# Late modulation vectors as row products, decay columns in the value block, token norms without VectorE

## The chip, the cores and the metric

The kernel runs on one core of a Trainium2 chip. Its time is device microseconds of one launch. Five engines work side by side, each through its own queue in order: TensorE (matmuls, transposes), VectorE, ScalarE, GpSimd, and SyncE (SP), which here only issues transfers. Data lie in HBM, in SBUF (128 partitions) and in PSUM, where matmuls accumulate.

## What is computed

One layer of a hybrid diffusion backbone on 512 latent tokens with 256 context tokens, D_MODEL 1024, float32 in and out:

```python
mod_lat = silu(c) @ w_mod + b_mod            # 6 vectors of 1024
sh1, sc1, g1, sh2, sc2, g2 = split(mod_lat, 6)
hx = rms_norm(x) * (1 + sc1) + sh1           # hc: the same of ctx, by mod_ctx
ak, av, qkv, db, da, aq, z, gate = split_cols(hx @ w_in)   # hc: the first five
attn = latent_attention(rope(rms(aq)), [k_ctx; k_lat], [v_ctx; v_lat])
q, k, v = silu(conv3(qkv)); q = l2(q) * 128**-0.5; k = l2(k)   # per head of 128
beta = sigmoid(db); log_a = -exp(a_log) * softplus(da + dt_bias)
gdn = rms(gated_delta_rule(q, k, v, log_a, beta), both directions) * silu(z)
y = sigmoid(g_a) * (attn @ w_pa) + sigmoid(g_d) * (gdn @ w_pd)
x = x + g1 * (y @ w_out)
h2 = rms_norm(x) * (1 + sc2) + sh2
u = conv3(h2 @ w_up); x = x + g2 * ((silu(u_g) * u_v) @ w_down)
out = rms_norm(x, final_norm_w)
```

The early vectors sh1 and sc1 are needed at once; g1, sh2, sc2 and g2 (4096 columns of w_mod, 16 MB) only from the output projection on: the late modulation vectors.

## The kernel before

Every large product is made of three fp32r matmuls (`mm3`): each operand is split into a high part (a copy on ScalarE, `whi`) and a low part (a subtraction on VectorE, `wlo`), and high x high, high x low and low x high are summed in PSUM. `load_w` loads a 128x1024 block of weights (512 KB, SP's queue) and splits it; it has three slots for split blocks.

The work runs in this order. (1) Up to 70 us: early modulation, norms and transposes of x and ctx, `hx` and `hc` (channels on partitions). (2) The key/value/query stage, `for blk in range(6)`: a 256-column block of keys (blk 0, six token tiles), of values (blk 1, six tiles), four of queries (four tiles each). A tile is 24 matmuls into `pq` with tokens on partitions; keys and queries then get their rope on VectorE and are transposed back (`columns`). Two side jobs are stepped in between: `next(mods)`, 2.6 steps per tile, and `next(dec)` at the tiles named in `DAT`. (3) Attention, with delta-rule projections between its steps. (4) The delta rule by four pairs of heads (`gdn_solve`, `gdn_inv`, `gdn_scan`), with projections, and from about 732 us the output projections `w_pa` and `w_pd`, woven in by rates (`weave`, `filler`). In a scan step the products `r` on VectorE stand between two groups of matmuls, and projection matmuls are put there as cover. (5) `w_out`, the MLP (`w_up`, `w_down`), the last norm.

TensorE's order is kept as written (`pinned`); that of other engines is set by a scheduler with priorities (`first`, `sooner`), except where `keep_in_program_order` is called.

`late_mods` (lines 367 to 399) takes the 4096 late columns in eight groups of 512 and each group in eight slices of 128 rows of w_mod: 64 loads of 256 KB. Odd slices are multiplied by silu(c) and summed on VectorE (`macc`, line 377), even ones scaled on ScalarE (line 379) and summed on GpSimd (line 381); `total` sums over the partitions with a matmul by ones, `columns` turns the 512 sums into four columns by one-row transposes, and VectorE adds the bias.

`decays` (line 596) projects `hc` and `hx` to the 32 columns db, da by 48 matmuls with the 32 weight columns as the stationary side, copies the result out (`grow`), transposes it by six tiles, and computes beta, the decays and their sums.

`tokens(h, part, src)` transposes a head's q, k or v to tokens on partitions; ScalarE squares and sums (`kss`). For q the factor `rkq` and for k the factors `rkk` and `hks` come from it: VectorE adds and scales, GpSimd raises to -1/2 (`rsqrt`), VectorE scales again. `hks` scales the v of the same head.

`finish_pa` and `finish_pd` apply the sigmoid gates to a chunk of 128 channels; `tdr` in HBM holds the gates and the first branch's result in between (store `tdr<-ga`).

Of the kernel before, what the change touches and what calls it, by code (L numbers as in the profile page):

```python
# [48 lines left out]
MV, MT, CT = 0, 6, 9  # L49
MACT, MK, MU = 1, 2.6, 0  # L50
MPIN, MB = 1, 5
DA = '11142332'
DAT = [(int(DA[i]), int(DA[i + 1])) for i in range(0, 8, 2)]
# [22 lines left out]
R_QW, R_QS, R_KW, R_KS, R_A, R_DT, R_END = 0, 128, 256, 384, 512, 528, 544  # L76


def hybrid_layer_body(tc, x, ctxt, xT, consts, cols, rows, w_mod1, w_mod2, w_db, w_aq, w_cm, w_pa, w_pd, w_out,
# [54 lines left out]
    with es:  # L134
# [27 lines left out]
        col = cp.tile([P, S_END + 120], F32, name="col")[:, 0:S_END]  # L162
# [5 lines left out]
        V.memset(mhalf, -0.5)  # L168
        mod = cr.tile([P, 48], F32, name="mod")
        modc = cp.tile([P, 16], F32, name="modc")  # L170
        csl = cp.tile([P, KT], F32, name="csl")
# [24 lines left out]
        def load_w(src, nk=KT, pool=None, bufs=OH):  # L196
# [3 lines left out]
            n = nk * P  # L200
# [85 lines left out]
        def tokens(h, part, src):  # L286
# [77 lines left out]
        def held(i):  # L364
            return tc.keep_in_program_order(i) if MPIN else i

        def late_mods():
            accs = {}

            def part(q, k):  # L370
                if k == 0:
                    accs[q] = [mdp.tile([P, 512], F32, name="macc", tag="macc", bufs=4) for _ in range(2)]
                av, ap = accs[q]
                wk = mdp.tile([P, 512], F32, name="wmd", tag="wmd", bufs=MB)
                SP.dma_start(wk, w_mod2[q, k // 2][:, (k % 2) * 512:(k % 2) * 512 + 512])
                if k % 2:
                    held(V.scalar_tensor_tensor(out=av, in0=wk, scalar=csl[:, k:k + 1], in1=av, op0=ALU.mult, op1=ALU.add))  # L377
                else:
                    held(A.activation((av, ap, wk)[min(k // 2, 2)], wk, AF.Copy, scale=csl[:, k:k + 1]))
                    if k > 2:  # L380
                        held(G.tensor_tensor(out=ap, in0=ap, in1=wk, op=ALU.add))
                if k == KT - 1:
                    held((V if MV else G).tensor_tensor(out=ap, in0=ap, in1=av, op=ALU.add))

            def total(q):
                ps = xbank()[0:1, :, :].rearrange("p a b -> p (a b)")
                mm(ps, ones[:, 0:1], accs[q][1])
                act(accs[q][0][0:1, :], ps)

            def columns(q):  # L390
                pst = xbank()[:, 0, 0:4]
                for i in range(4):
                    T.transpose(pst[:, i:i + 1], accs[q][0][0:1, i * P:(i + 1) * P], ident[0:1, 0:1])
                tt(mod[:, 16 + 4 * q:20 + 4 * q], pst, col[:, S_BMOD + 16 + 4 * q:S_BMOD + 20 + 4 * q], ALU.add)

            for i in range(9 * KT + CT - 7):
                for at, fn in ((MT, total), (CT, columns)):
                    q = (i - KT - at) // KT
                    if (i - at) % KT == 0 and 0 <= q < 8:
                        fn(q)  # L400
                if i < 8 * KT:
                    part(i // KT, i % KT)
                yield

        modact, mods = [MACT], late_mods()
# [14 lines left out]
        with m1_es:  # L420
# [38 lines left out]
            V.tensor_copy(csl, cs.rearrange("p (k two) -> p k two", two=2)[:, :, 0])  # L459
# [136 lines left out]
        def decays(g1):  # L596
            rowt = g1.tile([P, 32], F32, name="rowt")
            SP.dma_start(rowt, rows[R_A:R_END].partition_broadcast(P))
# [3 lines left out]
            raw = g1.tile([P, 256], F32, name="dbraw")  # L602
            SP.dma_start(raw, w_db)
            dbh = g1.tile([P, 256], F32R, name="dbh")
            dbl = g1.tile([P, 256], F32R, name="dbl")
            split(dbh, dbl, raw)
            grow = g1.tile([32, NA], F32, name="grow")
            for (xh, xl, n, off) in ((hcH, hcL, NCX, 0), (hxH, hxL, NL, NCX)):
                ps = mbank()[0:32]
                for k in range(KT):  # L610
                    mm3(ps[:, 0:n], dbh[:, k * 32:(k + 1) * 32], dbl[:, k * 32:(k + 1) * 32], xh[:, k, :], xl[:, k, :], k, KT)
# [990 lines left out]
```

## Time and profile before

| what | value |
|---|---|
| median of three runs | 1276.62 us (1276.61 to 1277.89) |
| profiled execution | 1276.79 us, its span 1275.0 us |
| TensorE matmul busy | 1217.5 us |
| VectorE busy | 849.0 us |
| ScalarE busy | 624.2 us |
| GpSimd busy | 308.5 us |

The times of the profile run from the span's start. PE is TensorE, PEld its loading of weights, DVE VectorE, ACT ScalarE, POOL GpSimd, SPq the queue of SyncE. A line number is that of kernel.py; most are those of small helpers, so groups go by the names of tiles.

### The profile page before, as it was taken

The page shows a single profiled execution, that of the slowest core. Times are in us where ns is not written, and L with a number is a line of the kernel's source. Part 1 is how long each engine was busy: PE and PEld are TensorE (multiplying, and loading weights), DVE is VectorE, ACT ScalarE, POOL GpSimd, SP SyncE. Part 2 cuts the span into 40 slices and gives each one's busy share as a digit, 9 for nine tenths or more (in the row PEclk, how much of TensorE's full clock was granted, in tenths as well). Part 3 has the DMA queues.
Part 4 walks back from the last instruction along what each step waited for, and adds up shares of the span by engine and source line. Part 5 has one row for each costly group of instructions (what it writes and reads, how often), then busy time and mean ns, then how long its engine had stood idle before and what let it go on. Part 6 is the DMA issues. An engine that isn't in the chain of part 4 may idle for free.

```text
span 1275.0 us, 20851 instructions
## 1 busy us (share of the span) xinstructions
PE 1217.5 (95%) x7835; PEld 1027.1 (81%) x7835; DVE 849.0 (67%) x1625; ACT 624.2 (49%) x1403; POOL 308.5 (24%) x364
## 2 busy tenths in 40 slices
PE   8899999999988899999999999999999999999996
PEld 4487878898877778778888888788988888888886
DVE  5886987777769985876665756565766666653333
ACT  5453657666666665474453543333444444442231
POOL 1753430000024348758547400000000000000000
PEclk8999999999999999999999999999999999999998
DMA  8656641111254643533543663464133222333321
GB/s 320 225 170 215 224 130 63 67 71 54 88 187 136 186 129 121 194 115 126 183 127 129 193 197 118 147 232 133 33 116 99 93 92 98 99 95 91 104 91 66
DMA packets 70788, 170.79 MB, mean 134 GB/s; under 512 B 7872, under 2 KB 18720, under 8 KB 69280
## 3 DMA queue, kind: packets, MB, share of 16 engines
q1 hardware_dynamic: 70688, 169.47, 40.3%
q8 instruction: 61, 1.00, 0.3%
q14 instruction: 39, 0.32, 0.1%
HBM read 144.23 MB, written 25.21 MB: 133 GB/s over the span
## 4 chain that ended last, share of the span: by engine, by line
PE 70%; DVE 12%; DMA 5%; ACT 3%; POOL 3%; issue 2%; SPq 0%; POOLq 0%; DVEq 0%; ACTq 0%
PE mc L87 32%; PE mb L87 20%; PE pb L87 5%; PE pq L87 3%; PE pS L87 3%; PE ab L87 3%; DVE wlo L108 2%; DMA Gb<-gamdr 2%; PE ab L91 1%; DMA M<-gamdr 1%; DVE macc L377 1%; PE pk L87 1%; PE xb L91 1%; DVE qt L108 1%; POOL prod L108 1%
## 5 line engine op out<-in xcount | busy, mean ns | idle before, releaser
L108 DVE TENSOR_TENSOR wlo<-wraw,whi 128x1024 fp32r<-128x1024 f32 x152 | 188.3, 1240 | 162.9 <-ACT whi L120 159.9
L120 ACT ACTIVATE whi<-wraw 128x1024 fp32r<-128x1024 f32 x152 | 158.8, 1047 | 208.4 <-PE mc L87 103.4
L87 PE MATMUL mc<-h,whi 128*128 128x512 f32 (+1 forms) x752 | 219.5, 376 | 0.3 <-ACT whi L120 0.3
L87 PE MATMUL mb<-hxH,whi 128*128 128x512 f32 x384 | 163.7, 426 | 2.6 <-DVE R L108 2.1
L87 PEld LDWEIGHTS mc<-h,whi 128*128 128x128 f32 x752 | 138.0, 188 | 26.0 <-ACT whi L120 0.5
L87 PE MATMUL mb<-hxH,wlo 128*128 128x512 f32 x384 | 153.7, 400 | 0.0
L87 PE MATMUL mb<-hxL,whi 128*128 128x512 f32 x384 | 153.0, 398 | 0.0
L87 PE MATMUL mc<-h,wlo 128*128 128x512 f32 (+1 forms) x376 | 141.3, 376 | 0.5 <-DVE wlo L108 0.5
L108 POOL TENSOR_TENSOR rc<-rc,mhalf 128x2 f32<-128x2 f32 x4 | 3.2, 811 | 452.3 <-DVE rc L114 452.3
L87 PE MATMUL mc<-a,whi 128*128 128x512 f32 (+1 forms) x396 | 111.1, 366 | 0.6 <-DVE x L117 0.6
L87 PEld LDWEIGHTS mb<-hxH,wlo 128*128 128x128 f32 x384 | 73.7, 192 | 17.0
L87 PEld LDWEIGHTS mb<-hxH,whi 128*128 128x128 f32 x384 | 74.0, 193 | 13.9 <-ACT t L120 2.3
L87 PEld LDWEIGHTS mb<-hxL,whi 128*128 128x128 f32 x384 | 74.3, 194 | 10.0
L87 PEld LDWEIGHTS mc<-a,whi 128*128 128x128 f32 x396 | 71.6, 189 | 12.9 <-DVE x L117 0.8
L87 PEld LDWEIGHTS mc<-h,wlo 128*128 128x128 f32 x376 | 70.8, 188 | 13.7 <-DVE wlo L108 1.0
L87 PE MATMUL mc<-a,wlo 128*128 128x512 f32 (+1 forms) x198 | 72.3, 365 | 0.0
L117 DVE SCALAR_TENSOR_TENSOR u<-mc,col,u 128x511 f32<-128x511 f32 x88 | 65.3, 746 | 1.4
L108 POOL TENSOR_TENSOR prod<-X,R 128x31 f32<-128x31 f32 (+15 forms) x93 | 55.4, 596 | 21.1 <-DVE X L108 14.3
L108 POOL TENSOR_TENSOR R<-R,prod 128x31 f32<-128x31 f32 (+15 forms) x93 | 54.9, 590 | 6.9
L87 PE MATMUL pq<-whi,hxH 128*128 128x256 f32 x192 | 55.3, 288 | 0.0
L87 PE MATMUL pq<-wlo,hxH 128*128 128x256 f32 x192 | 53.5, 279 | 0.2 <-DVE wlo L108 0.2
L87 PE MATMUL pq<-whi,hxL 128*128 128x256 f32 x192 | 53.4, 278 | 0.0
(346 smaller groups left out, 2859.4 us busy)
## 6 DMA issues: line engine op xcount, KB each, us to landing
wraw<-in_w_cm_dram SPq DMA_DIRECT2D x48, 512.0 KB, 4.1
wraw<-in_w_up_dram SPq DMA_DIRECT2D x44, 512.0 KB, 3.7
wmd<-in_w_mod_dram SPq DMA_DIRECT2D x64, 256.0 KB, 3.7
wm<-in_w_mod_dram SPq DMA_DIRECT2D x8, 1024.0 KB, 8.7
wraw<-in_w_down_dram SPq DMA_DIRECT2D x16, 512.0 KB, 3.6
wraw<-in_w_aq_dram SPq DMA_DIRECT2D x12, 512.0 KB, 4.7
M<-gamdr SPq DMA_DIRECT2D x64, 64.0 KB, 4.4
wraw<-in_w_pa_dram SPq DMA_DIRECT2D x8, 512.0 KB, 4.1
```

What stands on the lines that cost most here:

```text
L87: i = nc.tensor.matmul(*a, **k)
L91: i = nc.tensor.transpose(*a, **k)
L108: (eng or V).tensor_tensor(out=out, in0=a, in1=b, op=op)
L117: V.scalar_tensor_tensor(out=out, in0=a, scalar=s, in1=b, op0=op0, op1=op1)
L120: A.activation(out, a, f, **kw)
L377: held(V.scalar_tensor_tensor(out=av, in0=wk, scalar=csl[:, k:k + 1], in1=av, op0=ALU.mult, op1=ALU.add))
```

## The change

Three parts. `late_mods` is new: the weights are laid out transposed (`w_mod2[j]`: 128 output columns on partitions, 1024 inputs along the row), silu(c) is broadcast to all partitions (`cw`), and one VectorE instruction per 128 columns multiplies the two and gives the row's sum as a column of `ms`: 32 loads of 512 KB and 32 products. They are stepped from the output projections by `more_mods`, with rates .25 per head step in `w_pa`, .14 in `w_pd` and .25 per step in `w_out`, into a pool of its own (`lm`, two row buffers) that opens after `hx` closes.

The 32 columns db, da are put behind the 256 value columns: the value block is 288 wide, its weights come in three pieces (864, 864 and 576 columns), and columns 256 to 288 of each tile are copied to `psc`. The separate projection and its transposes are gone, and the steps of `decays` stand at other tiles.

In `tokens`, the additions and scalings are ScalarE's (Identity with scale and bias), `hks` is a power 1/2 on GpSimd, and the factor 128**-0.5 of q is put into the power. Besides, `finish_pd` has one addition on GpSimd instead of VectorE, and the tiles of `two` have another alignment.

```diff
-MV, MT, CT = 0, 6, 9
-MACT, MK, MU = 1, 2.6, 0
-MPIN, MB = 1, 5
-DA = '11142332'
+MPA, MPD, MPO = .25, .14, .25
+DA = '203242'
...
+        half6 = cpad[:, S_END:S_END + 6]
+        G.memset(half6, 0.5)
+        epss = {v: cpad[:, S_END + 6 + i:S_END + 7 + i] for i, v in enumerate((1.0, 4.0, 512.0))}
...
         def two(pool, k, by, name):
-            t = pool.tile([P, 2 * k * NL + 128], F32R, align_bytes=2048, name=name)
+            t = pool.tile([P, 2 * k * NL + 64], F32R, align_bytes=512, name=name)
...
                     if part != 2:
-                        rr = (rkq, rkk)[part][h]
-                        rsqrt(rr, kss[:, 0:n], 1.0, 4 * EPS)
+                        rr, q = (rkq, rkk)[part][h], (128.0, 1.0)[part]
+                        act(rr, kss[:, 0:n], AF.Identity, scale=q, bias=epss[4 * q])
+                        tt(rr, rr, mhalf[:, 0:n], ALU.pow, G)
                     if part == 1:
-                        stt(hks[h], kss[:, 0:n], 4 * EPS, rr, ALU.add, ALU.mult)
-                        ts(hks[h], hks[h], 0.5, ALU.mult)
-                    if part == 0:
-                        ts(rr, rr, 128.0 ** -0.5, ALU.mult)
+                        act(hks[h], kss[:, 0:n], AF.Identity, scale=0.25, bias=epss[1.0])
+                        tt(hks[h], hks[h], half6, ALU.pow, G)
...
+            SP.dma_start(cw, rows[R_C:R_END].partition_broadcast(P))
+            th = row()
+            act(th, cw, AF.Tanh, scale=0.5)
+            stt(cw, th, 1.0, cw, ALU.add, ALU.mult)
+            yield
+            for j in range(32):
+                wl = row()
+                SP.dma_start(wl, w_mod2[j])
+                tc.keep_in_program_order(V.scalar_tensor_tensor(out=wl, in0=wl, scalar=0.5, in1=cw, op0=ALU.mult, op1=ALU.mult,
+                                                                accum_out=ms[:, j:j + 1]))
+                if j % 8 == 7:
+                    tt(mod[:, 9 + j:17 + j], ms[:, j - 7:j + 1], col[:, S_BMOD + 9 + j:S_BMOD + 17 + j], ALU.add)
                 yield
...
+        def more_mods(rate):
+            mcount[0] += rate
+            while mcount[0] >= 1:
+                mcount[0] -= 1
+                next(mods, None)
...
-            raw = g1.tile([P, 256], F32, name="dbraw")
-            SP.dma_start(raw, w_db)
...
-                for k in range(KT):
-                    mm3(ps[:, 0:n], dbh[:, k * 32:(k + 1) * 32], dbl[:, k * 32:(k + 1) * 32], xh[:, k, :], xl[:, k, :], k, KT)
-                V.tensor_copy(grow[:, off:off + n], ps[:, 0:n])
-            yield
-            psc = flat(xbank())[:, 0:192].rearrange("p (a b) -> p a b", b=32)
-            for t in range(6):
-                T.transpose(psc[:, t, :], grow[:, t * P:(t + 1) * P], ident[0:32, 0:32])
+            psc = g1.tile([P, 6, 32], F32, name="psc")
+            yield psc
...
             for blk in range(6):
-                w2 = [load_w(w_aq[blk, i]) for i in range(2)]
+                if blk == 1:
+                    w2 = [load_w(w_av[:, 864 * i:864 * i + 288 * n], n=288 * n) for i, n in ((0, 3), (1, 3), (2, 2))]
+                else:
+                    w2 = [load_w(w_aq[max(blk - 1, 0), i]) for i in range(2)]
...
                     if blk == 1:
-                        split(VH[:, t, :], VL[:, t, :], pq)
+                        split(VH[:, t, :], VL[:, t, :], pq[:, 0:256])
+                        V.tensor_copy(psc[:, t, :], pq[:, 256:288])
                         continue
...
-            for _ in mods:
-                pass
...
             hx_es.close()
+            lmp.append(lm_es.enter_context(tc.tile_pool(name="lm", bufs=1, side="right", reuse_waits="tile")))
+            next(mods)
...
-                tt(gd, gd, ga, ALU.add)
+                tt(gd, gd, ga, ALU.add, G)
...
-        def head_gemm(ps, w, xs):
+        def head_gemm(ps, w, xs, rate):
             for h in range(NH):
                 while xs[h] is None:
                     yield
                 head_steps(ps, w, xs, h)
+                more_mods(rate)
                 yield
```

`paired` calls `more_mods(rate)` in the same way behind each `head_steps`, and `out_proj` calls `more_mods(MPO)` behind each of its eight steps.

## Rows read from the trace of the kernel before

**Rows 1.** The page: busy time, share of the span, instructions.

```profile
PE 1217.5 (95%) x7835; PEld 1027.1 (81%) x7835; DVE 849.0 (67%) x1625; ACT 624.2 (49%) x1403; POOL 308.5 (24%) x364
```

**Rows 2.** Windows by stage: length; PE, PEld, DVE, ACT, POOL busy; clock, DMA.

```profile
70.00:184.00 114.00, 107.40 (x829) 93.54 (x828) 99.45 (x260) 62.39 (x182) 45.93 (x34) 1.00 0.61 197
...
732.00:805.00 73.00, 71.99 (x498) 62.27 (x493) 43.22 (x94) 25.21 (x53) 0.00 (x0) 1.00 0.46 149
805.00:852.00 47.00, 46.24 (x203) 36.77 (x202) 28.95 (x47) 16.29 (x33) 1.64 (x1) 1.00 0.57 183
852.00:877.00 25.00, 25.00 (x111) 20.65 (x110) 13.80 (x19) 8.74 (x13) 0.00 (x0) 1.00 0.62 212
```

**Rows 3.** Chain of waits, 58 to 190 us: start, length, what (pieces of a kind).

```profile
70.48 5.77 PE pq L87 x48
...
97.82 8.29 PE mb L87 x48
...
108.83 0.95 PE xb L87 x2
109.77 2.94 PE pq L87 x24
112.71 0.33 PE xb L91 x4
...
115.98 0.48 PE xb L91 x6
...
172.75 0.22 PE pt L91 x2
...
183.50 0.44 PE pt L91 x2
```

**Rows 4.** Groups on VectorE, 70 to 184 us: busy us, mean ns, idle before.

```profile
L377 DVE SCALAR_TENSOR_TENSOR macc<-wmd,csl,macc 128x512 f32<-128x512 f32 x32 | 28.9, 908 | 1.1 <-DMA wmd<-in_w_mod_dram 1.1
```

**Rows 5.** Chain of waits, 758 to 770 us.

```profile
764.05 2.06 PE mb L87 x9
```

**Rows 6.** Waits of PE, 70 to 190 us: total us, times, longest.

```profile
PE pq L87 <- DVE wlo L108: 1.6, 2, 1.4
```

**Rows 7.** Groups on VectorE, 184 to 620 us: the forms behind the sums of q.

```profile
L112 DVE TENSOR_SCALAR rkq<-rkq 128x4 f32<-128x4 f32 x8 | 4.3, 543 | 6.6 <-POOL rkq L108 6.6
...
L114 DVE TENSOR_SCALAR rkq<-gkss 128x4 f32<-128x4 f32 x8 | 3.6, 455 | 12.7 <-ACT xb L120 12.7
```

**Rows 8.** Chain of waits, 345 to 700 us.

```profile
366.23 1.67 DVE hk L112
...
470.75 1.84 DVE rkq L114
```

**Rows 9.** Groups on ScalarE, 70 to 184 us.

```profile
L120 ACT ACTIVATION_READ_ACCUMULATOR qtmp<-pq 128x1 f32 x44 | 8.7, 197 | 0.0
```

**Rows 10.** Tile rkk: durations in ns, least/median/most, first and last start.

```profile
L108 POOL TENSOR_TENSOR rkk<-rkk,mhalf x8: 1321/1330/1971, 199.8 to 417.5; 128x6 f32<-128x6 f32 x8
```

**Rows 11.** Tile qt.

```profile
L108 DVE TENSOR_TENSOR qt<-qt,qtmp x20: 406/411/1506, 83.3 to 182.7; 128x256 f32<-128x256 f32 x20
```

**Rows 12.** Groups on VectorE, 805 to 852 us.

```profile
L108 DVE TENSOR_TENSOR wlo<-wraw,whi 128x1024 fp32r<-128x1024 f32 x8 | 9.8, 1220 | 2.9 <-ACT whi L120 2.9
L108 DVE TENSOR_TENSOR gd<-gd,ga 128x512 f32<-128x512 f32 x7 | 4.8, 689 | 0.2
```

**Rows 13.** Tile macc.

```profile
L377 DVE SCALAR_TENSOR_TENSOR macc<-wmd,csl,macc x32: 731/741/1705, 74.5 to 173.3; 128x512 f32<-128x512 f32 x32
```

**Rows 14.** Timeline of VectorE, 763 to 768 us: start, length, instructions.

```profile
763.87 1.11 DVE L117 SCALAR_TENSOR_TENSOR r<-pb,eg,vtok 128x128 f32<-128x128 f32 x4
```

**Rows 15.** The page's DMA issues: KB each, us to landing.

```profile
wraw<-in_w_pa_dram SPq DMA_DIRECT2D x8, 512.0 KB, 4.1
```

**Rows 16.** Waits of SP's queue, 690 to 880 us: total us, times, longest.

```profile
SPq L1246 <- DVE ga L117: 30.9, 7, 8.9
```

**Rows 17.** Groups on GpSimd, 70 to 184 us.

```profile
L383 POOL TENSOR_TENSOR macc<-macc 128x512 f32<-128x512 f32 x8 | 11.3, 1410 | 13.1 <-DVE macc L377 8.0 <-DVE qsc L114 5.0
```

More of the change, by code (lines that the diff above doesn't have):

```diff
@@ L48 @@
 NS = 2
-MV, MT, CT = 0, 6, 9
-MACT, MK, MU = 1, 2.6, 0
-MPIN, MB = 1, 5
-DA = '11142332'
-DAT = [(int(DA[i]), int(DA[i + 1])) for i in range(0, 8, 2)]
+MPA, MPD, MPO = .25, .14, .25
+DA = '203242'
+DAT = [(int(DA[i]), int(DA[i + 1])) for i in range(0, len(DA), 2)]
 KPIN, LAG, FQ = 1, 3, 0
@@ L75, with hybrid_layer_body @@
 S_BMOD, S_CW, S_FW, S_FB, S_GNW, S_FNW, S_C, S_END = 0, 48, 120, 252, 296, 297, 305, 321
-R_QW, R_QS, R_KW, R_KS, R_A, R_DT, R_END = 0, 128, 256, 384, 512, 528, 544
-def hybrid_layer_body(tc, x, ctxt, xT, consts, cols, rows, w_mod1, w_mod2, w_db, w_aq, w_cm, w_pa, w_pd, w_out,
+R_QW, R_QS, R_KW, R_KS, R_A, R_DT, R_C, R_END = 0, 128, 256, 384, 512, 528, 544, 1568
+def hybrid_layer_body(tc, x, ctxt, xT, consts, cols, rows, w_mod1, w_mod2, w_av, w_aq, w_cm, w_pa, w_pd, w_out,
                       w_up, w_down, outT, dbg=None):
@@ L161, in hybrid_layer_body @@
         msk_i = (cst[:, C_MI:C_MI + 128], cst[:, C_MI + 128:C_MI + 256])
-        col = cp.tile([P, S_END + 120], F32, name="col")[:, 0:S_END]
+        cpad = cp.tile([P, S_END + 128], F32, name="col")
+        col = cpad[:, 0:S_END]
         with sooner():
@@ L168, in hybrid_layer_body @@
         V.memset(mhalf, -0.5)
+        half6 = cpad[:, S_END:S_END + 6]
+        G.memset(half6, 0.5)
+        epss = {v: cpad[:, S_END + 6 + i:S_END + 7 + i] for i, v in enumerate((1.0, 4.0, 512.0))}
+        for v, t in epss.items():
+            G.memset(t, v * EPS)
         mod = cr.tile([P, 48], F32, name="mod")
         modc = cp.tile([P, 16], F32, name="modc")
-        csl = cp.tile([P, KT], F32, name="csl")
         def rsqrt(out, a, s, eps):
@@ L362, in gate_proj @@
                 SP.dma_start(tdr[c], o[:, 0:NL])
-        def held(i):
-            return tc.keep_in_program_order(i) if MPIN else i
         def late_mods():
[L368 to L402, printed above, removed]
-                yield
@@ L405, in hybrid_layer_body, with row @@
-        modact, mods = [MACT], late_mods()
+            cw = lmp[0].tile([P, D], F32, name="cw")
+            ms = lmp[0].tile([P, 32], F32, name="ms")
+            def row():
+                return lmp[0].tile([P, D], F32, name="wl", tag="wl", bufs=2)
+            SP.dma_start(cw, rows[R_C:R_END].partition_broadcast(P))
[10 more added lines that the diff above has]
+                    tt(mod[:, 9 + j:17 + j], ms[:, j - 7:j + 1], col[:, S_BMOD + 9 + j:S_BMOD + 17 + j], ALU.add)
+                yield
@@ L597, in decays @@
             rowt = g1.tile([P, 32], F32, name="rowt")
-            SP.dma_start(rowt, rows[R_A:R_END].partition_broadcast(P))
+            SP.dma_start(rowt, rows[R_A:R_C].partition_broadcast(P))
             trt = g1.tile([P, 2, P], F32, name="trt")
@@ L674, in hybrid_layer_body @@
         with kv_es:
-            mdp = kv_es.enter_context(tc.tile_pool(name="mdp", bufs=1, reuse_waits="tile"))
             kvp = kv_es.enter_context(tc.tile_pool(name="kvp", bufs=1, reuse_waits="tile"))
@@ L1246, in finish_pa @@
                 SP.dma_start(tdr[c], ga)
-            yield from paired(w_pa, 0, atn, finish_pa)
+            yield from paired(w_pa, 0, atn, finish_pa, MPA)
             for c in range(2, KT):
                 pa = mbank()
-                yield from head_gemm(pa, load_w(w_pa[c]), atn)
+                yield from head_gemm(pa, load_w(w_pa[c]), atn, MPA)
                 finish_pa(c, pa)
@@ L1263, in finish_pd @@
                 stt(gd, gd, 1.0, pd, ALU.add, ALU.mult)
-                tt(gd, gd, ga, ALU.add)
+                tt(gd, gd, ga, ALU.add, G)
                 act(yH[:, c, :], gd, AF.Copy, scale=0.5)
                 stt(yL[:, c, :], gd, 0.5, yH[:, c, :], ALU.mult, ALU.subtract)
-            yield from paired(w_pd, 0, gHL, finish_pd)
+            yield from paired(w_pd, 0, gHL, finish_pd, MPD)
             for c in range(2, KT):
                 pd = mbank()
-                yield from head_gemm(pd, load_w(w_pd[c]), gHL)
+                yield from head_gemm(pd, load_w(w_pd[c]), gHL, MPD)
                 finish_pd(c, pd)
@@ L1282, in head_gemm, with paired @@
                 head_steps(ps, w, xs, h)
+                more_mods(rate)
                 yield
-        def paired(w, c, xs, finish):
+        def paired(w, c, xs, finish, rate):
             two = [(mbank(), load_w(w[c + i])) for i in range(2)]
@@ L1291, in paired @@
                     head_steps(ps, wt, xs, h)
+                    more_mods(rate)
                     yield
@@ L1577, in _layout @@
     return a
-_ORDER = ["x", "ctxt", "xT", "consts", "cols", "rows", "w_mod1", "w_mod2", "w_db", "w_aq", "w_cm", "w_pa", "w_pd",
+_ORDER = ["x", "ctxt", "xT", "consts", "cols", "rows", "w_mod1", "w_mod2", "w_av", "w_aq", "w_cm", "w_pa", "w_pd",
           "w_out", "w_up", "w_down"]
```

40 lines of the change are left out of this document (17 added, 23 removed).

## The prediction

> **What bounds the kernel now.** I read the page's busy times first: TensorE's matmuls are busy 95% of the span, VectorE 67% [rows 1]. That alone says that only two things can give time: matmul work that goes away, and stretches in which TensorE waits. The windows by stage come next [rows 2]. In the key/value/query stage (70 to 184 us) the matmuls are busy 107.4 of 114 us, and VectorE is busy 99.5 of 114, nearly as much; in the three output projections, 732 to 877 us, TensorE is busy throughout and VectorE only 86.0 of 145. Third, the chain of waits for 70 to 184 us [rows 3]: which of its pieces are matmuls and what each costs; then VectorE's largest group there [rows 4]. What is left is to find, for the stages that receive work, the nearest instructions and the slack; these rows come with the parts below.
>
> **Late modulation, the part removed.** `late_mods` runs inside the key/value/query stage. Each group of 512 columns has a total (two half passes of a matmul, 0.95 us on the chain) and four one-column transposes (0.33 us) [rows 3]; eight groups make 8 x 1.28 = 10.2 us of TensorE. On VectorE go 32 products, 28.9 us [rows 4]. Sixty-four loads leave SP's queue there.
>
> **Decay and beta, moved into the value block.** The separate projection is 48 matmuls, 8.29 us of the chain, and six transposes, 0.48 us [rows 3]. In exchange six tiles of 24 matmuls get 288 columns instead of 256. A 256-column matmul takes 2.94/24 = 0.1225 us [rows 3], a 512-column one 2.06/9 = 0.229 us [rows 5]: 0.42 ns per column, so 32 x 144 columns are 1.9 us. Net 8.3 + 0.5 - 1.9 = 6.9 us.
>
> **The stage's sum.** It runs from 70.48 to 183.94 us, 113.5 us [rows 3]. Twenty-eight tiles at 2.94 are 82.3, 22 pairs of transposes at 0.22 are 4.8, the separate projection and its transposes 8.8, the modulation 10.2: 106.1 us. What is left, 7.3 us, is some 1 us of decay matmuls (my estimate) and waiting, as that of rows 6. After the change 10.2 + 6.9 = 17.1 us of matmul work are gone for certain. Of the waiting: VectorE's load falls from 99.5 to about 71 us (28.9 removed, six small copies added) over some 92 us, and ScalarE, at 62.4 of 114 [rows 2], gets less, so neither can bound the stage. I let 4.3 of the 7.3 us go and keep 2 us of stalls: gain 21.4 us. Bounds: 17.1 (all waiting stays) to 23.4 (only the decay matmuls stay). The kept 2 us are for the three-piece weights: the value block now fills all three slots of split weights, so the next block's first half can be split only when the value block's last tile has passed a third of its matmuls.
>
> **Token norms.** The add-and-scale in front of the power and the scalings behind it leave VectorE: the two forms for q alone are 3.6 and 4.3 us busy, with 12.7 and 6.6 us in which VectorE stood at them waiting for ScalarE or GpSimd [rows 7]. On the chain the pieces of all five forms add up to some 4.5 us in eight pieces, the two longest 1.67 and 1.84 us [rows 8]. ScalarE gets 24 small instructions behind its own accumulations, at about 0.2 us (the nearest row, its accumulator read, is 0.197 us [rows 9]); they wait for nothing but ScalarE, whose cover is matmuls as before, so I cost them at nothing, 4.8 us if all lay open. GpSimd gets eight more powers of 1.33 us [rows 10]. What is late next is the value head's scaling, which now waits for two powers in a row, 1.3 us later, in work that is issued several projection steps after its head. The gain lies between 4.5 us and, if two of the eight added powers hold up a VectorE instruction of the path, a loss of 2 x 1.33 = 2.7 us. I take 3 us gained: the chain's pieces less one such hold-up.
>
> GpSimd's price is visible before: with GpSimd at work a 0.41 us addition of two SBUF tiles took 1.51 us [rows 11]. The Trainium skill's page SBUF — State Buffer, section "SBUF: two separate sides", says that a VectorE instruction with two SBUF inputs and a GpSimd instruction that reads SBUF exclude each other for a whole instruction. By that rule, the trace agrees; with all eight new powers on the path the norms would lose 8 x 1.33 = 10.6 us instead of gaining 3.
>
> **Late modulation, the part added.** Thirty-two loads of 512 KB and 32 products of 128x1024 with an accumulated output, in the output projections. The trace has no such product. Nearest: the split's 128x1024 subtraction, 1.22 us [rows 12]; the 128x512 product, 0.741 us [rows 13]; an accumulator read on ScalarE, 0.197 us [rows 9]. Lower bound 1.22, upper bound at full rate 1.22 + 0.2 = 1.42; I take 1.35, nearer the upper one, since a product with a sum needs its read-out. The rates (0.25 and 0.14 of 64 head steps, then 0.25) place 16 in `w_pa`, 9 in `w_pd`, 7 in `w_out`. VectorE then has 43.2 + 21.6 = 64.8 of 73 us, 29.0 + 12.2 - 4.8 (seven additions of 0.69 us [rows 12] go to GpSimd in this window) = 36.4 of 47, and 13.8 + 9.5 = 23.3 of 25 [rows 2]. It fits everywhere, so the products hide under matmuls; the price is delay. Queued behind a product on VectorE are the scan's four `r` products and the split's `wlo`. A scan step covers 1.11 us of `r` [rows 14] with 2.06 us of projection matmuls [rows 5]: 0.95 us of slack against 1.35 us. A product that falls just there costs 0.4 us; I charge a quarter of that to each, 3.5 us in all. Bounds: 0, and the rivals (a) and (c) below. Without the cover it would be 32 x 1.35 = 43 us.
>
> SP's queue: a load of 512 KB lands in 4.1 us [rows 15]; a product is due every 73/16 = 4.6 us in `w_pa`, and with two buffers a load has about 8 us. The stores `tdr<-ga` hold SP for up to 8.9 us [rows 16]; a row's load behind one is late. That is rival (c).
>
> **The addition in `finish_pd` on GpSimd.** 1.41 us (the same addition of 128x512 there [rows 17]) instead of 0.69 us. Its last result is needed by the first output product's last eighth, 21 x 0.229 = 4.8 us after the last `w_pd` matmul; the sequence product, addition, copy, product is 1.41 + 3 x 0.69 = 3.5 us, if ScalarE's copy is like VectorE's addition. Cost nothing; 1.4 us if the cover goes. Alignments and memsets: nothing either way, since no row of the chain touches them.
>
> **Sum.** Against the profiled execution, 1276.8 us (span 1275.0 and 1.8 around it; the median of the three runs, 1276.6, is the same within 0.02%): -21.4 - 3 + 3.5 = -20.9, so 1255.9; I say 1256 us.
>
> **Rivals.**
> (a) Products at half rate: a 128x1024 product of two fp32 SBUF tiles with a sum might take 2 x 1.22 + 0.2 = 2.65 us. VectorE would need 85.6 of 73, 48.0 of 47 and 32.4 of 25 us: 21 us too much, in place of 3.5: 1273.5 us. Against it: the 128x512 product without a sum ran at the full rate [rows 13]; for it: no row has a sum on VectorE. 10%. The Trainium skill's Vector Engine (DVE) Microarchitecture Reference, section "7. Points that are easy to get wrong", states this halving of scalar-tensor-tensor with two sources in SBUF that aren't bf16, because no read port is left for the accumulator; without a sum the trace contradicts it, with one no row here shows.
> (b) The stage gains only its matmul work, and the borders cost: at the two borders of the value block a split (about 1.05 on ScalarE and 1.22 on VectorE) lies open. 17.1 - 4.6 = 12.5 us gained, 1265 us. For it: the wait for `wlo` [rows 6] is such a border. Against it: VectorE was late there with products that are gone. 15%.
> (c) Slower. The place is VectorE in `w_pa`: row loads queue behind `tdr<-ga` on SP, a product stands at the head of VectorE's queue until its row lands, and the scan and the splits stand behind it. With all 30.9 us of those waits [rows 16] passed on to TensorE: 1276.8 - 24.4 + 30.9 = 1283 us. It decides from 24.4/32 = 0.76 us per product. Against it: a row's load waits for nothing but its buffer, so it can stand ahead of the stores. 5%.
> (d) No effect: the removed work wasn't on the path, and the stage stays at 113 us: 1277 us. Against it: its matmul pieces are on the chain themselves. 4%.
> The forecast: 66%.
>
> **Range and chances.** The forecast's own range is 1249 (23.4 + 4.5 gained, rows free) to 1263 (17.1 gained, norms nothing, rows at 3.5). Taken up to (b) with its products at 0.25 us each it is 1249 to 1270, which leaves out (a), (c) and (d). A change within 0.2% (2.6 us) can't be told from none. Faster: 66 + 15 + 4 (of a) = 85%; same: 4 (of a) + 3 (of d) = 7%; slower: 5 + 2 (of a) + 1 (of d) = 8%.
>
> **What would show it.** Right: the stage from the first `pq` matmul to the first score lasts 90 to 94 us, with VectorE busy under 75 us in it; a value tile takes 3.2 to 3.3 us; products take 1.2 to 1.45 us; TensorE is busy over 97% from the first `w_pa` matmul to the last of `w_out`. Wrong: products of 2 us and more; VectorE idle in front of them until a load lands; TensorE waiting for `r` or `wlo` after 700 us; a stage that still takes over 100 us.

## The result and the profile after

The changed kernel took 1266.16 us (median of 4 runs, 1261.5 to 1267.7); the kernel before, on the same chip, 1277.26. The ratio is 0.991, 95% interval 0.9885 to 0.9935. The change saves 11.1 us; the forecast was 20.9. The profiled execution has a span of 1264.3 us. On the page, TensorE lost 14 us of busy time and VectorE only 4:

```profile
PE 1203.2 (95%) x7733; PEld 1023.3 (81%) x7733; DVE 844.9 (67%) x1609; ACT 608.5 (48%) x1388; POOL 300.0 (24%) x360
```

Where the time went is read by cutting both spans at the same five events: the first `pq` matmul, the first score, the first matmul of `w_pa`, that of `w_up`, and the end. Before: 70.3 us, then 113.4, 548.8, 165.3 and 377.2. After: 69.1, 90.3, 547.3, 180.9 and 376.9. So the key/value/query stage gave 23.1 us, the output projections took 15.6 back, and the rest moved by 3 us in all.

The first of these, in the windows by stage (length; PE, PEld, DVE, ACT, POOL busy; clock, DMA), answers to the first row of [rows 2]: matmuls 107.4 to 87.1 us, VectorE 99.5 to 65.0.

```profile
69.00:159.30 90.30, 87.07 (x724) 86.21 (x724) 64.99 (x223) 38.60 (x140) 16.14 (x14) 0.99 0.25 82
```

Its chain of waits (start, length, what) shows a value tile, the border behind the value block, and a query tile. Under it stand the window of that border and TensorE's only listed wait in the stage (us, times, longest):

```profile
86.95 3.17 PE pq L85 x24
...
104.16 1.07 ACT whi L118
...
105.25 1.24 DVE wlo L106
...
137.06 2.74 PE pq L85 x24
```

```profile
104.00:107.00 3.00, 2.95 (x23) 2.74 (x23) 1.79 (x3) 2.39 (x3) 0.00 (x0) 1.00 0.00 0
```

```profile
PE pt L89 <- DVE QL L106: 3.1, 1, 3.1
```

The value tile with 288 columns takes 3.17 us. At the border, for which the prediction kept 2 us, the split of the next block's weights is on the chain for 1.07 + 1.24 us, but TensorE hardly stands: it is busy 2.95 of 3 us there with the value block's last tile. It stands 3.2 us in the stage, 3.1 of them at its end, where the transposes of the last query tile wait for VectorE. And a query tile takes 2.74 us where the prediction's took 2.94 [rows 3].

The chain of the whole stage, shares by engine, tile and line, before (70.48 to 183.94 us; the view cuts its line off) and after (69.06 to 159.33 us):

```profile
by line: PE pq L87 32.1%; DVE macc L377 10.8%; DVE qt L108 9.0%; PE mb L87 7.5%; issue 6.9%; DVE qtmp L108 5.6%; DVE wlo L108 5.2%; DMA wraw<-in_w_cm_dram 2.9%; PE xb L91 1.9%; PE xb L87 1.7%; PE pt L91 1.6%; DVE s L108 1.3%; POOL rk L108 1
```

```profile
by line: PE pq L85 86.7%; PE pt L89 5.6%; DVE wlo L106 2.7%; ACT whi L118 2.4%; PE mb L85 1.0%; DVE qtmp L106 0.6%; DVE QL L106 0.4%; DVE qt L106 0.4%; issue 0.3%; PE xb L89 0.1%; DVE qsc L112 0.1%
```

Before, the chain ran over VectorE for 47.8 of 113.5 us and over TensorE for 51.0; after, over TensorE for 84.2 of 90.3 us. By this chain VectorE was as much a limit of the stage before as TensorE; the lines that [rows 3] shows are TensorE's alone.

Then the three output projections, `w_pa`, `w_pd` and `w_out`, after, and under them their sum in the kernel before (same cuts):

```profile
706.60:785.90 79.30, 74.08 (x484) 62.19 (x481) 62.38 (x131) 25.73 (x55) 0.00 (x0) 1.00 0.79 259
785.90:836.40 50.50, 46.84 (x204) 36.92 (x203) 39.95 (x62) 16.29 (x33) 11.19 (x7) 1.00 0.82 276
836.40:887.50 51.10, 48.33 (x276) 42.11 (x275) 33.74 (x57) 17.02 (x29) 4.13 (x3) 0.93 0.54 185
sum 180.90, PE 169.26 PEld 141.22 DVE 136.07 ACT 59.04 POOL 15.31; mean PE 56.42 PEld 47.07 DVE 45.36 ACT 19.68 POOL 5.10
```

```profile
sum 165.30, PE 163.53 PEld 139.61 DVE 98.23 ACT 57.41 POOL 2.62; mean PE 54.51 PEld 46.54 DVE 32.74 ACT 19.14 POOL 0.87
```

In `w_pa` VectorE is busy 62.4 of 79.3 us, by no means full, and yet TensorE stands for 5.2 us there, and for 11.6 us in all three (1.8 before). The other 5.7 us of the loss are matmuls that were busy for longer; 3.2 of them lie in `w_out`, where the clock is 0.93. Windows of 5 us, the first two in `w_pd`, the rest around the start of `w_out`, show how:

```profile
810.00:815.00 5.00, 2.73 (x13) 1.94 (x12) 2.50 (x5) 1.06 (x1) 1.27 (x1) 1.00 1.00 352
815.00:820.00 5.00, 5.00 (x23) 4.11 (x22) 4.60 (x6) 1.96 (x3) 2.18 (x2) 1.00 0.86 277
...
835.00:840.00 5.00, 5.00 (x23) 4.11 (x22) 4.53 (x7) 1.69 (x2) 1.51 (x2) 1.00 0.82 312
840.00:845.00 5.00, 2.23 (x7) 1.14 (x7) 5.00 (x6) 0.63 (x1) 1.91 (x1) 0.83 0.93 296
845.00:850.00 5.00, 5.00 (x14) 3.84 (x13) 2.64 (x6) 1.78 (x3) 0.00 (x0) 0.50 1.01 357
850.00:855.00 5.00, 5.00 (x23) 4.15 (x22) 1.64 (x2) 1.75 (x3) 0.00 (x0) 0.99 0.73 291
```

At 840 us TensorE stands 2.8 us while VectorE is busy throughout; then the granted clock is 0.50, the lower of its two levels (1.2 GHz), for 5 us, and 14 matmuls fit where 23 did. `w_out` is 6.0 us longer than before, 2.8 of standing and 3.2 of slower matmuls: the wait is paid about twice. That is not so of every stall: after 2.3 us of standing at 811 us the clock stayed at 1.00. What tells the two apart is not shown.

Two of the stalls, at 754 and at 840 us, in the timeline of VectorE, GpSimd and TensorE (in brackets, how long the engine had stood and for what):

```profile
754.84 1.23 DVE L382 SCALAR_TENSOR_TENSOR wl<-wl,cw 128x1024 f32<-128x1024 f32 x1 [2.20 <-DMA wl<-in_w_mod_dram]
...
755.99 1.12 DVE L115 SCALAR_TENSOR_TENSOR r<-pb,eg,vtok 128x128 f32<-128x128 f32 x4
...
756.49 0.68 PE L85 MATMUL pb<-r,TTm 128*128 128x128 f32 x4 [1.66 <-DVE r L115]
```

```profile
839.79 2.12 POOL L106 TENSOR_TENSOR gd<-gd,ga 128x512 f32<-128x512 f32 x1 [1.82 <-issue]
...
840.71 1.75 DVE L115 SCALAR_TENSOR_TENSOR y<-gd,y 128x512 fp32r<-128x512 f32 x1
...
842.51 0.50 PE L85 MATMUL mc<-y,whi 128*128 128x512 f32 x1 [2.08 <-DVE y L115]
```

The first is a late row: the product waits for it, the scan's `r` products stand behind the product, and TensorE behind `r`. The 2.3 us at 811 us are of the same kind, with the gate's product `gd` in place of `r`. At 840 us no row is late: rows' products, the last two gated chunks and a split follow one another on VectorE without a gap, and one step of `y` takes 1.75 us beside GpSimd's addition.

The products themselves (durations in ns min/median/max; then what VectorE waited for in front of them, us and times; then the loads, issue to landing):

```profile
L382 DVE SCALAR_TENSOR_TENSOR wl<-wl,cw x32: 1210/1218/2318, 715.3 to 857.1; 128x1024 f32<-128x1024 f32 x32
L382 DVE DVE_READ_ACCUMULATOR wl<-wl,cw x32: 74/81/85, 716.4 to 858.2; 128x1 f32 x32
...
  DMA wl<-in_w_mod_dram: 11.4, 8
...
DMA to landing us min/median/max: 3.3/4.5/9.0
```

1.22 + 0.08 = 1.30 us each, as forecast (1.35): rival (a) is out. But in eight places VectorE stood in front of a product, 11.4 us in all, until the row had landed.

### The profile page after: what moved, and what is told of

Same layout as the page of the kernel before. It is cut to its first block, busy times and chain, and to the rows that moved or that the text cites. A ratio compares the mean times of both kernels' runs of the same rounds, so it can differ in the third digit from the quotient of the medians.

```text
span 1264.3 us, 20518 instructions
## 1 busy us (share of the span) xinstructions
PE 1203.2 (95%) x7733; PEld 1023.3 (81%) x7733; DVE 844.9 (67%) x1609; ACT 608.5 (48%) x1388; POOL 300.0 (24%) x360
## 4 chain that ended last, share of the span: by engine, by line
PE 71%; DVE 8%; DMA 6%; POOL 4%; ACT 3%; issue 3%; SPq 0%; POOLq 0%; DVEq 0%; ACTq 0%
PE mc L85 32%; PE mb L85 18%; PE pq L85 6%; PE pb L85 5%; PE pS L85 3%; PE ab L85 3%; DMA wl<-in_w_mod_dram 2%; DVE wlo L106 2%; PE ab L89 1%; POOL prod L106 1%; POOL R L106 1%; PE pk L85 1%; PE xb L89 1%; POOL NN L106 1%; DMA NN<-gamdr 1%
## 5 line engine op out<-in xcount | busy, mean ns | idle before, releaser
L106 DVE TENSOR_TENSOR wlo<-wraw,whi 128x1024 fp32r<-128x1024 f32 (+1 forms) x153 | 193.0, 1262 | 159.7 <-ACT whi L118 159.1
L118 ACT ACTIVATE whi<-wraw 128x1024 fp32r<-128x1024 f32 (+1 forms) x153 | 159.7, 1044 | 213.7 <-PE mc L85 109.3
L106 POOL TENSOR_TENSOR prod<-X,R 128x31 f32<-128x31 f32 (+15 forms) x93 | 54.4, 585 | 20.4 <-DVE X L106 13.6
L85 PE MATMUL pq<-whi,hxH 128*128 128x256 f32 (+1 forms) x192 | 55.4, 288 | 0.0
L85 PE MATMUL pq<-wlo,hxH 128*128 128x256 f32 (+1 forms) x192 | 54.2, 282 | 0.1
L85 PE MATMUL pq<-whi,hxL 128*128 128x256 f32 (+1 forms) x192 | 54.0, 281 | 0.0
```

Of the source, the lines that this page charges most:

```text
L85: i = nc.tensor.matmul(*a, **k)
L106: (eng or V).tensor_tensor(out=out, in0=a, in1=b, op=op)
L118: A.activation(out, a, f, **kw)
```

## The experiments

Twelve runs, in four jobs on different chips (c0 is the changed kernel once more); the kernel before had medians of 1274.3 to 1276.8 us in them, so each is compared with the runs of its own job. "Gain" is the median less that of before; the other columns are from the cut profiles, in us, to 0.1: from first score to `w_pa`, the three output projections, and from `w_up` on.

| kernel | gain | ratio, 95% interval | to `w_pa` | output proj. | rest |
|---|---|---|---|---|---|
| before | | | 548.8 | 165.3 | 377.2 |
| after | -11.1 | 0.991 (0.9885 to 0.9935) | 547.3 | 180.9 | 376.9 |
| c0_after_again | -9.8 | 0.9927 (0.9911 to 0.9944) | 547.8 | 181.7 | 376.9 |
| e1_no_rows | -26.5 | 0.98 (0.978 to 0.982) | 549.1 | 165.6 | 376.4 |
| e2_loads_only | -25.0 | 0.9825 (0.9801 to 0.9848) | 543.3 | 169.8 | 377.0 |
| e3_products_only | -18.7 | 0.9865 (0.9842 to 0.9888) | 545.8 | 175.9 | 376.4 |
| e4_gd_vector | -13.9 | 0.9901 (0.9884 to 0.9919) | 544.9 | 180.2 | 376.5 |
| e6_pool_queue | -0.3 | 0.9995 (0.9975 to 1.0016) | 549.1 | 186.3 | 376.9 |
| e7_halves | -10.1 | 0.9927 (0.9907 to 0.9947) | 544.8 | 181.3 | 376.9 |
| e8_norms_undone | -10.5 | 0.9918 (0.9895 to 0.9942) | 543.5 | 182.2 | 377.1 |
| b1_no_late_mods | -19.4 | 0.9843 (0.9818 to 0.9867) | 547.2 | 164.2 | 376.9 |
| f1_spread_rows | -12.5 | 0.9896 (0.9873 to 0.9919) | 552.8 | 174.7 | 377.0 |
| f2_spread_rows_add | -9.7 | 0.9929 (0.991 to 0.9949) | 560.1 | 171.0 | 376.8 |
| g1_rows_moved | -13.3 | 0.9897 (0.9867 to 0.9927) | 546.3 | 175.8 | 376.9 |

The stretch up to `w_pa` ranges over 6 us (543 to 549) among kernels that are the same there; a difference of a profile below that, in that column, is not evidence. `w_pa` by itself ranges nearly as far among kernels with the same rows in it (79.3 us after, 78.7 in c0, 82.2 in e4, 83.5 in e8), while their sums for the three output projections agree within 2 us. The first two kernels' stage of keys, values and queries is in the text above; it is 89.7 to 90.3 us in all others but b1.

**What the rows cost, and which half of them.** Four kernels of one job.

e1 drops the load and the product, e2 the product; both take the bias alone for the late vectors. e3 drops the load and multiplies `cw` by itself, the last line below in the product's place.

```diff
-                SP.dma_start(wl, w_mod2[j])
-                tc.keep_in_program_order(V.scalar_tensor_tensor(out=wl, in0=wl, scalar=0.5, in1=cw, op0=ALU.mult, op1=ALU.mult,
...
+                tc.keep_in_program_order(V.scalar_tensor_tensor(out=wl, in0=cw, scalar=0.5, in1=cw, op0=ALU.mult, op1=ALU.mult,
```

> Left out: the 32 row loads and the 32 products of the late modulation; the late vectors are the bias alone. Whatever the cause, this gives what the rows cost in the output projections. The milestones of the changed kernel's trace put all that is lost after 706 us at 15.6 us; if the rows are all of it, 1266.2 - 15.6 = 1250.6 us (1249 to 1253). If the addition on GpSimd and the general state of the stage cost part of it, 1254 to 1260. If my 3.5 us for the rows was right and the loss is elsewhere, 1262 to 1263.

> The 32 row loads stay, the products are left out (late vectors are the bias alone), so nothing on VectorE waits for a row. Theory 1 (VectorE stands in program order in front of a product until its row has landed): the cost goes, 1250 to 1253 us, as without rows. Theory 2 (the products' 1.3 us each fill VectorE): also 1250 to 1253. Theory 3 (16 MB more through the DMA engines delay the weight and tdr loads): most of the cost stays, 1260 to 1266 us.

> The 32 products stay, with the same operand twice from SBUF in place of a loaded row; the 32 loads are left out (the late vectors are wrong). Theory 1 (waiting for the row): the cost goes but for my 3.5 us, 1253 to 1256 us. Theory 2 (the products' own time on VectorE): most of the cost stays, 1260 to 1266 us. Theory 3 (DMA traffic): 1250 to 1254.

Without rows the output projections are back at 165.6 us, with `w_pa` as before:

```profile
707.90:781.00 73.10, 72.62 (x482) 62.21 (x481) 45.58 (x100) 25.81 (x54) 0.00 (x0) 1.00 0.48 159
781.00:828.60 47.60, 46.58 (x203) 36.91 (x202) 28.42 (x40) 16.68 (x34) 13.35 (x8) 1.00 0.55 182
828.60:873.50 44.90, 44.90 (x275) 40.24 (x274) 26.23 (x44) 15.96 (x28) 2.28 (x2) 1.00 0.46 153
```

So the rows are the whole loss: 15.3 us by the stages, 15 to 17 by the runs (26.5 against 11.1 and 9.8). GpSimd's addition is in e1 and, with no products beside it, can have cost no more than the 0.5 us of `w_pd` there. By the stages the products alone take 10.3 us (175.9 less 165.6) and the loads alone 4.2; by the runs 7.8 and 1.5. Both theories 1 and 2 are therefore half right, and theory 3 a little: the largest single part is VectorE's time in products that wait for nothing. What the two cost only together, the waiting for landings among it, is 1 us by the stages and 7 by the runs; the measurements don't settle it more closely. Nor is e2 half of the changed kernel: with no product to hold a buffer it starts 27 of its 32 loads in `w_pa`, the changed kernel 18. The windows of `w_pa` with the loads alone, and of `w_pa` and `w_pd` with the products alone, show the two means: DMA share 0.92, and VectorE 44.1 of 50.6.

```profile
702.40:778.20 75.80, 73.09 (x483) 62.04 (x482) 45.30 (x96) 25.84 (x55) 0.00 (x0) 1.00 0.92 329
```

```profile
704.50:782.10 77.60, 74.13 (x483) 62.46 (x481) 60.94 (x127) 25.58 (x54) 0.00 (x0) 1.00 0.45 150
782.10:832.70 50.60, 48.46 (x204) 38.10 (x204) 44.10 (x65) 16.83 (x34) 15.16 (x8) 0.97 0.51 172
```

**The addition in `finish_pd`.**

```diff
-                tt(gd, gd, ga, ALU.add, G)
+                tt(gd, gd, ga, ALU.add)
```

> The addition of finish_pd back on VectorE, the rest as in the changed kernel. Prediction: no difference, 1266 us. Rival theory 4 (GpSimd's eight additions of about 1.6 us hold up VectorE's two-input instructions for as long; in the changed trace the splits and products beside them took 1.8 to 2.3 us in place of 1.2): 3 to 6 us faster, 1260 to 1263 us.

The median, 1262.8 us, lies where the rival theory put it. The gain is 13.9 against 11.1 and 9.8: 3 to 4 us, but with intervals that overlap, and by the stages of the one profile 0.7 (180.2 against 180.9). The mechanism can be seen, its price is not settled. In the changed kernel two products, three splits and the one `y` above took 1.75 to 2.35 us beside GpSimd's additions instead of 0.68 to 1.22; in the group of the products by tile, none is slow any more with the addition back:

```profile
L382 DVE SCALAR_TENSOR_TENSOR wl<-wl,cw x32: 1211/1218/1227, 713.2 to 856.7; 128x1024 f32<-128x1024 f32 x32
```

**Why a row is late, and whether its length matters.**

```diff
-                SP.dma_start(wl, w_mod2[j])
+                G.dma_start(wl, w_mod2[j])
...
-                return lmp[0].tile([P, D], F32, name="wl", tag="wl", bufs=2)
+                return lmp[0].tile([P, D // 2], F32, name="wl", tag="wl", bufs=4)
```

The first is e6, the second e7, which also halves the product, doubles the rates and adds the two half sums.

> The 32 row loads are issued from GpSimd's queue, which is idle in w_pa, instead of SP's; all else as in the changed kernel. If rows land late because their loads stand behind the waiting tdr stores on SP (rival c of the prediction), and because weights stand behind waiting row loads, the idle time of VectorE in front of the products (11.4 us) falls to 2 to 4 us and the time to 1257 to 1261 us. If two buffers set the lead (a load can start only when the product two rows before is done, whatever queue issues it), nothing: 1264 to 1268 us.

> Each row product in two halves: 64 loads of 256 KB and 64 products of 128x512, four buffers of half the size, twice the rate; the same bytes in the same SBUF. A half product should take 0.62 + 0.08 = 0.7 us, VectorE 45 us in place of 42. If what costs is the length of one product in front of a product r, a split or a y (1.3 us against 0.95 us of slack), most of the products' own share of the cost goes: 1258 to 1261 us. If it is the sum of VectorE's work, or the waiting for landings, no gain: 1265 to 1269 us.

On GpSimd's queue the waiting in front of products stays at 9.6 us. The kernel loses 10 us against the changed one, which neither expectation foresaw; `w_pa` takes 79.2 us, as in the changed kernel, so the loss lies elsewhere, and its cause is open. The new queue's own waits say why the queue is not the cause of late rows: 61.4 us of them are for the product two rows before, that is for a buffer (the view by tile: what the engine that issues or computes waited for, us and times).

```profile
  DVE wl L382: 61.4, 22
...
  DMA wl<-in_w_mod_dram: 9.6, 8
...
DMA to landing us min/median/max: 3.6/4.6/7.3
```

In the changed kernel the same stands in SP's waits:

```profile
SPq L381 <- DVE wl L382: 32.0, 19, 3.9
```

The trace of the changed kernel says the same row by row. Of the 30 loads behind the first two, 24 were issued within 0.04 us of the end of the product that freed the buffer, then took 3.3 to 9.0 us to land. Products don't come evenly: two often start 1 to 3 us apart, and the next then finds its row still on the way. Of the eight late rows SP's order delayed one, by 2.2 us behind a load from `tdr`. Whether the weights behind a waiting row came late isn't shown.

Half products change nothing that can be measured (gain 10.1; 8.8 us of waiting in ten places; output projections 181.3), so the length of one product is not the main cost. A third whole buffer doesn't fit in SBUF beside the output projections, so a longer lead was not tried.

**The parts that should gain.**

b1 is made of the kernel before; e8 has `tokens` as the kernel before has it, the rest as after.

```diff
-        modact, mods = [MACT], late_mods()
+        modact, mods = [MACT], iter(())
...
-                        act(rr, kss[:, 0:n], AF.Identity, scale=q, bias=epss[4 * q])
-                        tt(rr, rr, mhalf[:, 0:n], ALU.pow, G)
+                        rsqrt(rr, kss[:, 0:n], 1.0, 4 * EPS)
```

> The kernel before without its late modulation (late vectors are the bias alone), with the separate decay and beta projection and the old norms. The prediction's terms: 10.2 us of matmul work plus a part of the 4.3 us of waiting, 1262.4 to 1266.4 us. If the stage gained 24 to 25 us in all because VectorE was its real limit (99.5 of 114 us busy), more than that: 1259 to 1262 us.

> The token norms as before (add and scale on VectorE, one power on GpSimd, products on VectorE behind it), the rest as in the changed kernel. The prediction's term: 3 us slower, 1269 us. Bounds of it: 1263.5 (the added powers cost more than they save) to 1270.7 us. From the milestones of the two traces, which gained no more between the first score and the last rkq power than measurement noise of 1 to 2 us: 1265 to 1268 us.

Without the late modulation the stage is 96.9 us; its window, with the decay projection still separate:

```profile
69.00:166.10 97.10, 93.85 (x779) 89.82 (x778) 65.43 (x219) 38.41 (x141) 16.15 (x14) 0.99 0.21 71
```

So the late modulation was worth 113.4 - 96.9 = 16.5 us there (TensorE's busy time fell from 107.4 to 93.9 us, its standing by 3) and the decays 96.9 - 90.3 = 6.6. The whole program gains 19.4, 3 us more than the stage, within what the profiles differ by elsewhere, but more than both expectations of b1; the one by which VectorE was the stage's limit is the nearer. b1 takes TensorE's pieces and VectorE's 32 products away together, so it doesn't tell which of the two engines decided.

With the old norms the gain is 10.5 against 11.1 and 9.8, and the stretch that holds them takes 543.5 us, at the lower edge of the nine kernels with new norms and no rows in that stretch (543.3 to 549.1, mean 546.5; the three with old norms: 548.8, 547.2, 543.5, mean 546.5). The new norms gain nothing that can be measured; the intervals of the runs don't exclude a few us. The windows of that stretch, after and e8:

```profile
159.30:706.60 547.30, 521.90 (x4058) 452.42 (x4056) 398.10 (x783) 332.60 (x883) 237.20 (x310) 0.98 0.38 127
```

```profile
159.10:702.60 543.50, 519.47 (x4058) 449.93 (x4056) 405.60 (x823) 326.27 (x859) 223.88 (x302) 0.99 0.37 127
```

VectorE does have 7.5 us less work, as the change says; ScalarE has 6.3 more and GpSimd 13.3 more.

**Does the price go with the density of rows, or with the place?** In f1, 12 rows are taken, as halves, beside the z and gate projections in a pool of their own, 12 in `w_pa` and `w_pd`, and the last eight, which only the final residual reads, are loaded into the weights' own buffers beside `w_up`. In f2 it is 16, 8 and 8, with the addition on VectorE. g1 has 16 in `w_pa`, 8 in `w_pd` and 8 beside `w_up`, and the addition on VectorE. All three have these lines:

```diff
...
+                up(ci, load_w(w_up[ci]), slice(0, NL))
+                more_mods(MPU)
```

> The changed kernel once more, unchanged, for the comparison with the other kernels of this job: 1261 to 1268 us, a ratio of 0.988 to 0.994.

> The rows spread over stages with more room: 12 rows, as half products of 128x512, beside the z and gate projections (500 to 690 us); 12 whole rows in the three output projections in place of 32; the last 8 (the vector that only the final residual needs) beside w_up. If the cost of the rows comes from their density in the output projections (VectorE's time and the waiting for landings, 15.9 us for 32 rows), 12 rows there cost 12/32 of it or less and the others nearly nothing: 1250.3 + 6 = 1256 us (1252 to 1259). If a row costs 0.5 us wherever it stands, because VectorE holds something up in each stage: 1264 to 1268 us as the changed kernel.

> As the kernel with spread rows, with 16 rows beside the z and gate projections, 8 in the output projections and 8 beside w_up, and the addition of finish_pd on VectorE again. By density: 8/32 of 15.9 us is 4 us, 1254 us (1250 to 1257), with 0 to 3 us less for the addition. If the half products in the z and gate stage hold up the solve, which has GpSimd at work beside it, 1258 to 1266 us.

The expectation by density is wrong: spreading gains 1 to 3 us in f1 and nothing in f2. The cut profiles tell the price by place. Beside the z and gate projections, where the delta rule's solve runs, 12 rows cost 552.8 - 546.5 = 6.3 us and 16 rows 13.6, both beyond the range of 543 to 549. In the output projections 12 rows still cost 9.1 us and 8 rows 5.4 (over 165.6), more for each than 32 do (each by one profile). Beside `w_up` eight rows cost nothing: 376.7 to 377.0 us against 376.4 to 377.2 without. Density alone doesn't explain the difference: g1 has a row every 21.8 us there, f2 one every 17 us beside the solve. In the windows (f2: up to `w_pa`, then from `w_up` on; e1 for the same two) VectorE has 27 us more work in the first and is busy 426 of 560 us, and in the last 10 us more at no cost:

```profile
158.60:718.70 560.10, 524.60 (x4059) 453.88 (x4057) 426.22 (x853) 333.78 (x884) 245.95 (x310) 0.98 0.41 140
889.70:1266.50 376.80, 366.67 (x1760) 309.07 (x1758) 208.39 (x299) 143.45 (x199) 2.26 (x3) 0.99 0.32 102
```

```profile
158.80:707.90 549.10, 521.69 (x4059) 451.98 (x4057) 399.33 (x780) 332.48 (x882) 237.51 (x310) 0.98 0.37 126
873.50:1249.90 376.40, 366.16 (x1760) 308.77 (x1759) 198.69 (x280) 142.85 (x198) 2.27 (x3) 0.99 0.28 91
```

> No row in w_out: 16 rows in w_pa and 8 in w_pd as in the changed kernel, the last 8 beside w_up (where 8 rows cost nothing in the kernel with spread rows), and the addition of finish_pd on VectorE. If a row costs by its place (from the stages of the runs so far: 16 rows in w_pa some 6 us, 8 in w_pd 3 to 4, none in w_out and w_up): 1250.3 + 9.5 = 1260 us (1257 to 1262), 6 us under the changed kernel. If each row costs 0.5 us in whatever stage: 1266 us. If the addition on VectorE costs what a row does, 1263 us.

The last kernel moves rows to where they are free. Its `w_out` is at 44.9 us again, at full clock, where the changed kernel has 51.1:

```profile
785.80:836.60 50.80, 46.83 (x204) 36.91 (x203) 37.69 (x65) 16.82 (x34) 1.64 (x1) 1.00 0.74 248
836.60:881.50 44.90, 44.90 (x275) 40.26 (x274) 26.10 (x45) 16.06 (x28) 0.70 (x1) 1.00 0.42 148
881.50:1258.40 376.90, 366.66 (x1760) 309.16 (x1758) 207.85 (x297) 142.52 (x198) 2.27 (x3) 0.99 0.32 102
```

It is surely faster than the kernel before. Its stage `w_pd` is as long as after (50.8 against 50.5 us). Against the changed kernel it has the better median (1261.0 against 1266.2 and 1265.9 us; gain 13.3 against 11.1 and 9.8) and output projections 5 us shorter, but the intervals overlap: a likely improvement of 2 to 5 us, not a proven one. And it isn't shown to come from the moved rows: e4, with the addition on VectorE and every row where the changed kernel has it, gains 13.9.

## Why the prediction came out as it did

The forecast was 1256 us, the range 1249 to 1270, and 1266 lies in it. The direction and the source of the gain were right; the forecast itself missed by 10 us, almost all of it one term, the price of the rows. By steps:

- **The stage of keys, values and queries: the size right, the path only half.** 23.1 us against 21.4, in the bounds of 17.1 to 23.4. The decays gave 6.6 for 6.9. The late modulation gave 16.5, where 10.2 of matmuls and up to 4.3 of waiting had been counted. The sum took the stage as a row of matmul pieces, 106.1 of 113.5 us, and asked of VectorE only whether it could bound the stage afterwards. The chain before ran over TensorE for 51 us and over VectorE for 48, and a tenth of the whole chain was the modulation's products (`macc`). Both engines were nearly full and lost work together, so the sum came out; that is in part luck. The 2 us kept for the border are about what TensorE still stands (3.2), but it stands at the stage's end and not at the border.
- **Token norms: mis-sized.** 3 us forecast, nothing measured (e8), though 3 us are within the intervals. VectorE's work fell by 7.5 us, ScalarE's and GpSimd's rose by 19.6 together; that the new pieces took the place of the old ones on the chain is likely, but not shown. Nor did the added powers cost the 10.6 us that stood as the worst case.
- **The rows: the term that failed, in two steps.** 3.5 us forecast, 15 to 17 measured. The durations were right (1.30 us for 1.35). Wrong was first the charge of a quarter of 0.4 us to each product (32 of them are 3.2 us, not 3.5): it priced one product against one gap in the scan and let everything between be hidden. e3 shows 0.32 us for each product by the stages and 0.24 by the runs, with no row to wait for. Wrong was second "with two buffers a load has about 8 us", which holds for products at even distances: the load is issued only when the product two rows before is done, lands 3.3 to 9.0 us later, and eight products stood waiting. The loads alone cost 1.5 to 4.2 us, a term that the sum did not have at all. No step counted the clock, which made 6 us of a stall of 2.8 in `w_out`. And the prediction's window for `w_out` ends at 877 us, the stage at 897.8; its seven products there were five, with 16 in `w_pa` and 11 in `w_pd`.
- **Rival (c)** had named the right place (a product at the head of VectorE's queue until its row lands) and 0.76 us as the price from which the change would lose; the price was 0.5. Its cause, the order on SP, holds for one of the eight late rows; for six it was the freeing of the buffer, and the first has no row before it. In e6, with the loads off SP, as many rows are late.
- **Rival (a)** is refuted by the products' rows: 1.218 us, against 1.22 for the split's subtraction [rows 12]. By the rule of the Trainium skill's Vector Engine (DVE) Microarchitecture Reference, section "7. Points that are easy to get wrong", it would have been half the rate; for fp32 with a sum this trace does not agree.
- **Rival (b)** came to 1265 us, near the measured time, by another way: it charged the stage, which paid in full.
- **The addition on GpSimd at nothing:** open. By e4 it costs 3 to 4 us in the medians and 0.7 in the stages. Its sequence did not stay under its cover as reckoned: from the last `w_pd` matmul (836.1 us) to the last `y` (844.2 us) it took 8.1 us, where 3.5 had been set against 4.8 of cover, because products stood between its steps and steps took longer beside each other.
- **What would show it:** stage 90.3 us with VectorE under 75, value tile 3.17, products 1.30: as written. TensorE over 97% in the output projections: 169.3 of 180.9 is 94%, and VectorE's idle time in front of products, as well as TensorE's waiting for `r` (2.7 us), were named as signs of an error.

## What to carry to other kernels

An engine's free share does not price work that is put on it: the same row, load and product, cost 0.5 to 0.9 us beside a chain of dependent steps (solve, scan, gate) and nothing beside `w_up`. The likely reason, not tested by itself, is that there TensorE works on weights that were split ahead. So price added work by what stands next in that engine's queue, and put it where that is farthest from being needed. A streamed operand needs its buffers counted from the end of the instruction that frees them to the landing of the next load, at the landing time of the stage with the new traffic in it. And look for a stage in which two engines are nearly full: most of the gain here was the late modulation, taken out of a stage in which TensorE was busy 94% and VectorE 87%, and it had pieces on both. A chain of waits has to be read with all engines in it before its pieces are added up.

## What the runs showed of the hardware

- A short stall of TensorE can be followed by a stretch at 1.2 GHz: 2.8 us idle, then 5 us at 0.50 and 14 matmuls in place of 23. Kernels without stalls in that stretch (e1, g1 in `w_out`) show 1.00 there. Another stall, 2.3 us at 811 us, was followed by 1.00.
- VectorE's product of two 128x1024 fp32 tiles with a sum runs as fast as the plain subtraction, and reads its sum out in 0.08 us, while ScalarE takes 0.2 us for that [rows 9].
- Beside GpSimd's 128x512 additions such products took up to 2.32 us, with the additions on VectorE at most 1.23. Additions and splits that meet slow each other: two additions (1.29 us alone) took 3.52 us together and two subtractions (1.22 us alone) 4.22, as the timeline of the changed kernel shows below. The rule that the prediction cited from the Trainium skill, SBUF — State Buffer, section "SBUF: two separate sides", fits that.
- Loads that no instruction waits for seem to cost time too: with them the DMA share in `w_pa` is 0.92, and that stage took 75.8 us against 73.1 without rows; by the runs it is 1.5 us, hardly clear of noise.

```profile
800.26 3.52 POOL L106 TENSOR_TENSOR gd<-gd,ga 128x512 f32<-128x512 f32 x2 [8.84 <-DVE gd L115]
...
800.64 4.22 DVE L106 TENSOR_TENSOR wlo<-wraw,whi 128x1024 fp32r<-128x1024 f32 x2
```
